# Sparse attention of a two-layer trunk: float32 matmuls replaced by three float16 passes over high and low parts, two heads per pass on the two halves of the rows

## Chip, cores, metric

One core of one Trainium2 chip runs the whole program. The metric is device time in microseconds of one execution, lower is better. Engines are named as in the profile: PE (TensorE matmul), PEld (its weight loads), DVE (VectorE), ACT (ScalarE), POOL (GpSimd), SP (SyncE, which here issues most DMAs).

## The reference, cut to what matters

A trunk of two layers over 512 rows of width 1024, in float32. Each layer has a mixing part with two branches (an RWKV-7 recurrence and a sparse attention), a cross-attention into 256 memory rows, and a feed-forward part (dense in layer 0, 8 experts in layer 1). The change touches the sparse attention alone:

```python
# q: 512 rows x 8 heads x 64, k and v: one head of 64; q_idx: 8 indexer heads x 64, k_idx: 64, w_idx: 8
def query_block(i):                      # 128 queries at a time
    limit = ((start + arange(128)) // 64 + 1) * 64       # keys before limit may be seen
    logits = einsum('bqhd,bsd->bqhs', q_idx, k_idx) * 64 ** -0.5
    score = einsum('bqhs,bqh->bqs', relu(logits), w_idx) * 8 ** -0.5
    score = where(key_pos < limit, score, -1e30)
    sel = top_k(score, 128)              # top_k = min(256, 512 // 4)
    s = einsum('bqhd,bqkd->bqhk', q, k[sel]) * 64 ** -0.5
    p = softmax(where(sel < limit, s, -1e30))
    return einsum('bqhk,bqkd->bqhd', p, v[sel])
```

In the mixing part the recurrence's output and the attention's output are each projected (`w_branch_a`, `w_branch_b`), gated, added and projected again (`w_out`).

## The kernel before

The 512 rows are four tiles of 128 partitions. Weights come in tiles of 512 KB (`raw`), are split into two float16 parts (`whi` by ACT, `wlo` by DVE, line 268, or by POOL, line 266) and multiplied in three float16 passes (high by high, low by high, high by low; `proj_feat`, line 285, tile `pf`, moving 128x512; `proj_tok2`, line 345, tile `ptok`). The recurrence and the sparse attention compute in float32.

**The mixing part** is written as Python generators that `layer` steps through in an order given by a string (`ORDER`): `r` the recurrence, `d` keys and queries, `s` the selection, `a` the attention, `g` gates (16 pf projections), `b` branch projections. A scheduler with a model of the engines then puts the instructions of each engine into their final, static order, so work of all generators is mixed. Every engine runs its own list in that order; an instruction that waits holds up those behind it on the same engine.

**The recurrence** (`rwkv`) handles heads in two groups of four. For each group: `rwkv_mats` (pA, line 793, on PE; AM, line 797, on DVE), `rwkv_inverse` (the block to DRAM and back, `scrA<-AM`, `Bt<-scrA`; a row-by-row inverse on DVE, pr and tt, lines 971 and 972; products pr and z, x, lines 988 and 990; then pY, line 1013, Ys, line 1016, and pX, line 1022), and `rwkv_chain` (pH, pG, pMQ, and then eight steps in which PE computes pSy, line 889, and DVE scales the new state TT, line 897, twice a step; the next step needs TT). `rwkv_out` ends a group (pyT, line 927; pg, line 940; r, line 941). In the trace the second group's inverse follows the first group's chain.

**The sparse attention** (`dsa`). `keys_queries` projects, normalises and rotates, transposes on PE and copies the results out of PSUM into kT, ikT (keys, indexer keys) and qT, iqT (queries). All have 64 numbers per head on the partitions, and two copies or two heads in the two halves of the 128 rows. For each block b of 128 queries, with n = 128 (b+1) keys:
- `select` (b = 1 to 3): per indexer head one matmul pl (line 503, contracting 64 rows, moving n columns), ACT's relu (line 505), DVE's weighted sum into iacc (lines 507, 509); then 16 rounds of top-8 on DVE (MAX8, line 513, and MATCH_REPLACE8, line 514), and the mask (line 515).
- `attend`, called for the two halves jp of the heads and for the parity e of the head: two matmuls psc (line 529), DVE's masked row maximum (line 530), nb (531), ACT's exponential with row sum (534), DVE's rv (536), ACT's scaling (538); after a yield the probabilities are transposed on PE (pp, line 546), copied out (pT, line 547, by ACT or DVE), and multiplied with v (po, line 553). With e = 1 the result is split into ybh, ybl (lines 200, 201) and stored to DRAM (`ybd`). Once all are stored, `branches` loads `yb<-ybd` and runs the pf of `w_branch_b`.

PSUM banks: two are shared by pl, psc, pp and pk (tag `att`), one holds po, two serve pf and ptok.

Of the kernel before, what the change touches and what calls it, by code (L numbers as in the profile page):

```python
# [54 lines left out]
class Kern:  # L55
# [315 lines left out]
    def dsa(self, l, hh, hl, ybd, cx):  # L371
# [68 lines left out]
        def attends():  # L440
            todo = []
            for b in range(NT):
                if b == 0:
                    c2 = ExitStack()
                    dw = pool("dsav", 1, c2)
                if b == 2:
                    next(todo.pop(0), None)
                    c2.close()
                    c1.close()
                    dw = pool("dsaw", 2, cx)  # L450
                for jp in range(2):
                    for e in range(2):
                        todo.append(self.attend(dw, b, jp, e, masks[b], qT, kT, vt, qs, ybd))
                        next(todo[-1])
                        if len(todo) > 1:
                            next(todo.pop(0), None)
# [4 lines left out]

    def queries(self, pp, hh, hl, c, c0, dst, tabs, qs):
# [3 lines left out]
        for cc in range(2):  # L466
            ps = self.proj_tok2([c(c0 + 256 * cc, c0 + 256 * cc + 256)], hh, hl)
            for i in range(2):
# [18 lines left out]
                nc.scalar.copy(dst[:, 2 * cc:2 * cc + 2, 2 * i * P:(2 * i + 2) * P].rearrange("p j (t c) -> p t j c", t=2),  # L487
                               pt.rearrange("p (t j c) -> p t j c", t=2, j=2))

    def select(self, dw, b, m, iqT, ikT, iw):  # L490
# [9 lines left out]
        for h in range(8):  # L500
            hs = slice((h % 2) * 64, (h % 2) * 64 + 64)
            pl = self.bank("att", "pl")
            nc.tensor.matmul(pl[:, :n], lhsT=iqT[hs, h // 2, bs], rhs=ikT[hs, :n], start=True, stop=True)  # L503
# [13 lines left out]
    def attend(self, dw, b, jp, e, mask, qT, kT, vt, qs, ybd):  # L517

        nc = self.nc
        n = (b + 1) * P  # L520
# [4 lines left out]
        mx, nb, sm, rv = (dw.tile([P, 2], F32, name=x, bufs=2) for x in ("mx", "nb", "sme", "rv"))
        q2 = qs[:, b, 4 * jp + e:4 * jp + e + 3:2]
        for i in range(2):
            pl = self.bank("att", "psc")
            nc.tensor.matmul(pl[:, :n], lhsT=qT[es, 2 * jp + i, bs], rhs=kT[es, :n], start=True, stop=True)  # L529
            nc.vector.tensor_tensor_reduce(s2[:, i, :n], pl[:, :n], mask, 1.0, -3.0e38, OP.add, OP.max, mx[:, i:i + 1])  # L530
        nc.vector.scalar_tensor_tensor(nb, mx, -1.0, q2, OP.mult, OP.mult)
        for i in range(2):
            h = 4 * jp + 2 * i + e
            nc.scalar.activation(s2[:, i, :n], s2[:, i, :n], AF.Exp, bias=nb[:, i:i + 1], scale=qs[:, b, h:h + 1],
                                 accum_out=sm[:, i:i + 1])
        nc.vector.reciprocal(rv, sm)
# [3 lines left out]
        pT = dw.tile([P, nm // P, 2 * P], F32, name="pT", bufs=1)  # L540
        for k2 in range(0, b + 1, 2):
            m = min(2, b + 1 - k2)
            pp = self.bank("att", "pp")
            for x in range(2 * m):
                kt = k2 + x // 2
                nc.tensor.transpose(pp[:, x * P:(x + 1) * P], s2[:, x % 2, kt * P:(kt + 1) * P], self.ident)
            (nc.scalar.copy if k2 == 0 else nc.vector.tensor_copy)(
                pT[:, k2:k2 + m, :], pp[:, 0:2 * m * P].rearrange("p (k c) -> p k c", k=m))
        if e == 0:
            self.po = self.bank("po", "po")  # L550
        po = self.po
        for kt in range(b + 1):
            nc.tensor.matmul(po[es, 0:2 * P], lhsT=vt[:, kt, :], rhs=pT[:, kt, :], start=kt == 0, stop=kt == b)  # L553
        if e == 1:
            yh = dw.tile([P, 2, P], F16, name="ybh")
            yl = dw.tile([P, 2, P], F16, name="ybl")
            self.split_ps(yh, yl, po[:, 0:2 * P].rearrange("p (j t) -> p j t", j=2))
            for d, y in zip(ybd, (yh, yl)):
                nc.sync.dma_start(d[2 * jp:2 * jp + 2, :, bs].rearrange("j p t -> p j t"), y)
# [1184 lines left out]
```

## Time and profile before

| what | value |
|---|---|
| median of 3 runs | 2145.76 us (2144.34 to 2150.21) |
| the profiled execution, its own time | 2149.16 us |
| its span in the trace | 2147.3 us |
| mean granted PE clock | 0.96 |
| busy PE, DVE, ACT, POOL | 2006.6, 1379.4, 1011.8, 334.8 us |
| psc (529) on PE, busy | 48.9 us, 128 records of 64 matmuls |
| pl (503) on PE, busy | 50.7 us, 96 records of 48 matmuls |
| po (553) on PE, busy | 44.4 us, 160 records of 80 matmuls |
| pp (546) on PE, busy | 27.7 us, 160 records |

A float32 matmul leaves two records on PE. Busy times of PE overlap, since matmuls are pipelined and their ends are modelled: the distance from one start to the next says what a matmul costs the queue. "Released by" names the work that an engine waited for. The profile's own time exceeds its span by 1.9 us, work outside the trace's first and last instruction.

### The profile page before, as it was taken

Reading aid. Unit: us, or ns where it says so; the run is one execution under the profiler, and the core shown is the slowest. Engines: PE = TensorE matmul, PEld = TensorE weight load, DVE = VectorE, ACT = ScalarE, POOL = GpSimd, SP = SyncE. Lnnn points to the kernel's source line nnn. Section 1 sums busy time; section 2 is a strip of 40 time slices with the busy share of each in tenths; the row PEclk is TensorE's granted clock in tenths of the full one; section 3 lists DMA queues with packets and bytes.
Section 4 is the critical chain, followed back from the end, with each engine's and each line's share of the span. In section 5 each row is a group of like instructions: output and inputs, shape, how many; then the busy total and the mean of one; then the engine's idle time right before and its main releaser. Section 6 shows DMA issues by size and latency. Waiting matters only on the chain.

```text
span 2147.3 us, 40225 instructions
## 1 busy us (share of the span) xinstructions
PE 2006.6 (93%) x16520; PEld 1310.3 (61%) x16520; DVE 1379.4 (64%) x2322; ACT 1011.8 (47%) x1617; POOL 334.8 (16%) x354
## 2 busy tenths in 40 slices
PE   7998999988998999999999988999798799999997
PEld 4664455555464544444583555546455699999996
DVE  6767984555665433322567787464655698888886
ACT  5533344542453333322443344543233488888883
POOL 2261601003010000000252260101100220000002
PEclk9998989999999999999999889999999799999998
DMA  7333323352542333333333231435330899999993
GB/s 226 102 90 83 105 75 90 71 162 88 197 157 63 98 103 104 99 106 100 115 89 84 82 108 48 116 81 178 116 122 27 287 386 374 356 352 344 345 346 120
DMA packets 346706, 332.47 MB, mean 155 GB/s; under 512 B 101889, under 2 KB 263809, under 8 KB 346514
## 3 DMA queue, kind: packets, MB, share of 16 engines
q1 hardware_dynamic: 335408, 306.03, 45.3%
q10 hardware_dynamic: 8482, 15.39, 2.1%
q0 software_dynamic: 2624, 8.40, 1.1%
q8 instruction: 131, 2.15, 0.4%
q14 instruction: 61, 0.50, 0.1%
HBM read 297.05 MB, written 32.72 MB: 154 GB/s over the span
## 4 chain that ended last, share of the span: by engine, by line
PE 70%; DVE 15%; DMA 5%; issue 3%; ACT 2%; SPq 2%; POOL 1%; another core or an unknown queue 0%; ACTq 0%; DVEq 0%; POOLq 0%
PE pf L285 20%; PE pe L1513 12%; PE ptok L327 10%; PE py L1558 6%; PE ptok L345 3%; PE pf L297 3%; PE pSy L889 3%; DVE iacc L514 2%; DVE m L513 2%; DVE wlo L268 2%; PE po L553 1%; PE psc L529 1%; PE pl L503 1%; DVE pr L988 1%; PE pA L793 1%
## 5 line engine op out<-in xcount | busy, mean ns | idle before, releaser
L263 ACT ACTIVATE whi<-raw 128x1024 f16<-128x1024 f32 (+3 forms) x242 | 227.0, 940 | 438.7 <-PE pf L285 195.2
L268 DVE SCALAR_TENSOR_TENSOR wlo<-raw,whi 128x1024 f16<-128x1024 f32 (+3 forms) x208 | 233.7, 1125 | 215.3 <-ACT whi L263 202.4
L1499 DVE SCALAR_TENSOR_TENSOR ewlo<-eraw,ewhi 128x1024 f16<-128x1024 f32 x265 | 321.4, 1222 | 59.4 <-ACT ewhi L1498 58.2
L285 PEld LDWEIGHTS <-whi 128*128 128x128 f16 x1888 | 181.8, 98 | 242.3 <-issue 43.5
L1498 ACT ACTIVATE ewhi<-eraw 128x1024 f16<-128x1024 f32 x265 | 277.2, 1053 | 81.3 <-PE py L1558 34.5
L1513 PE MATMUL pe<-XT,ewhi 128*128 128x144 f16 x2816 | 207.3, 227 | 2.5 <-ACT XT L200 2.3
L1513 PEld LDWEIGHTS <-ewhi 128*128 128x128 f16 x2816 | 184.2, 98 | 3.1 <-issue 2.5
L285 PE MATMUL pf<-hh,whi 128*128 128x512 f16 x448 | 170.8, 381 | 5.6 <-ACT qe L481 2.0
L285 PE MATMUL pf<-hl,whi 128*128 128x512 f16 x448 | 170.9, 382 | 0.0
L285 PEld LDWEIGHTS <-wlo 128*128 128x128 f16 x944 | 92.9, 100 | 113.0 <-issue 12.4
L285 PE MATMUL pf<-fh,whi 128*128 128x512 f16 x336 | 127.3, 379 | 0.0
L285 PE MATMUL pf<-fl,whi 128*128 128x512 f16 x336 | 127.3, 379 | 0.0
L1513 PE MATMUL pe<-XT,ewlo 128*128 128x144 f16 x1408 | 117.7, 227 | 0.2 <-issue 0.2
L285 PE MATMUL pf<-hh,wlo 128*128 128x512 f16 x448 | 116.2, 392 | 0.0
L1558 PE MATMUL py<-HT,ewhi 128*128 128x144 f16 x1408 | 104.0, 227 | 0.0
L164 POOL TENSOR_TENSOR rs<-rs,nrm_e 128x1 f32<-128x1 f32 x28 | 17.5, 625 | 520.4 <-DVE rs L163 520.4
L266 POOL TENSOR_TENSOR wlo<-raw,whi 128x1024 f16<-128x1024 f32 (+3 forms) x34 | 59.2, 1741 | 241.2 <-ACT raw L265 205.2
L1513 PEld LDWEIGHTS <-ewlo 128*128 128x128 f16 x1408 | 95.0, 98 | 0.6 <-issue 0.6
L1558 PEld LDWEIGHTS <-ewhi 128*128 128x128 f16 x1408 | 92.5, 98 | 0.3 <-issue 0.2
L285 PE MATMUL pf<-fh,wlo 128*128 128x512 f16 x336 | 79.4, 379 | 0.0
L345 PE MATMUL ptok<-whi,hh 128*128 128x256 f16 (+1 forms) x320 | 78.8, 285 | 0.0
L345 PE MATMUL ptok<-whi,hl 128*128 128x256 f16 (+1 forms) x320 | 78.5, 284 | 0.0
(435 smaller groups left out, 3863.3 us busy)
## 6 DMA issues: line engine op xcount, KB each, us to landing
raw<-in_w_in_dram SPq DMA_DIRECT2D x76, 512.0 KB
eraw<-in_moe_wg_dram SPq DMA_DIRECT2D x16, 2048.0 KB
eraw<-in_moe_wu_dram SPq DMA_DIRECT2D x16, 2048.0 KB
eraw<-in_moe_wd_dram SPq DMA_DIRECT2D x16, 2048.0 KB
eraw<-in_moe_wg_dram SPq DMA_DIRECT2D x8, 1536.0 KB
eraw<-in_moe_wu_dram SPq DMA_DIRECT2D x8, 1536.0 KB
eraw<-in_moe_wd_dram SPq DMA_DIRECT2D x8, 1536.0 KB
raw<-in_ffn_wg_dram SPq DMA_DIRECT2D x22, 512.0 KB
```

What stands on the lines that cost most here:

```text
L263: nc.scalar.activation(hi, raw, AF.Copy, scale=SW)
L266: nc.gpsimd.tensor_tensor(lo, raw, hi, OP.subtract)
L268: nc.vector.scalar_tensor_tensor(lo, raw, SW, hi, OP.mult, OP.subtract)
L285: self.nc.tensor.matmul(p, lhsT=w[:, k, :], rhs=x[k], start=first, stop=last)
L297: m = self.nc.tensor.matmul(ps[i][:, cs], lhsT=w[:, k, :], rhs=x[k][:, cs], start=hf == 0 and start, stop=stop, skip_group_check=True)
L327: mm(ps[t][:, :N], lhsT=x[:, k0 + k, ts], rhs=w[:, k, :], start=k0 == 0 and first, stop=k0 + kg == kt and last)
L345: mm(p, lhsT=x[:, k0 + k, ts], rhs=w[:, k, :], start=k0 == 0 and t % 2 == 0 and first, stop=k0 + kg == kt and last, skip_group_check=True)
L889: m = mm(p[e][:, cc % 4, jj, :], lhsT=l, rhs=r, start=first[e] is None, stop=x == (1 if cc else 0), skip_group_check=True)
L1498: nc.scalar.activation(r[0], w, AF.Copy, scale=SW)
L1499: nc.vector.scalar_tensor_tensor(r[1], w, SW, r[0], OP.mult, OP.subtract)
L1513: mm(p[:, i * n:(i + 1) * n], lhsT=w[:, k, :], rhs=XT[:, k, h, :], start=z == 0, stop=z == len(ms) - 1)
L1558: mm(ps[d], lhsT=w[:, i, d * P:(d + 1) * P], rhs=HT[:, k, h, :], start=k == 0 and w is wh and h == 0 and d % per == 0, stop=k == FT - 1 an ...
```

## The change

Every operand of the attention's matmuls is kept as two float16 tiles, high and low (`kT[0]`, `kT[1]` and so on), the same bytes as before. `split_ps` writes them: ACT casts the high part out of PSUM, DVE subtracts it and writes the low part. Scores come from a new function `scores` for two heads at once: three passes (high by high, low query by high key, high query by low key), and in each pass one matmul for each parity e, whose 64 rows are the upper or the lower half of the array, into two PSUM banks. `select` uses it for pairs of indexer heads. `attend` handles four heads in one call (both parities); its probabilities are scaled by 64 (`SP`), v by 64 (`SW`), and po is accumulated in three passes with the two parities in turn, each into its half of the output partitions. The tile s2 becomes s4 (four heads, two buffers), pT becomes four float16 tiles.

```diff
-        kT = dp.tile([P, SEQ], F32, name="kT")
-        vt = dp.tile([P, NT, 64], F32, name="vt")
+        two = lambda p, n, *s: [p.tile([P, *s], F16, name=n + x) for x in "hl"]
+        kT = two(dp, "kT", SEQ)
+        vt = two(dp, "vt", NT, 64)
...
-                    nc.scalar.copy(kT[:, cs]..., pv[:, :, 0, :])
-                    nc.vector.tensor_copy(ikT[:, cs]..., pv[:, :, 1, :])
+                    for g, dst in enumerate((kT, ikT)):
+                        self.split_ps(*[d[:, cs]... for d in dst], pv[:, :, g, :])
...
-                nc.scalar.copy(dst[:, 2 * cc:2 * cc + 2, ...], pt...)          # queries: iqT and qT
+                self.split_ps(*[d[:, 2 * cc:2 * cc + 2, ...] for d in dst], pt...)
...
         for h in range(8):                                                     # select
-            pl = self.bank("att", "pl")
-            nc.tensor.matmul(pl[:, :n], lhsT=iqT[hs, h // 2, bs], rhs=ikT[hs, :n], start=True, stop=True)
+            if h % 2 == 0:
+                pls = self.scores(iqT, h // 2, bs, ikT, n)
+            pl = pls[h % 2]
...
+    def scores(self, qT, j, bs, kT, n):
+        pls = [self.bank("att", "psc") for _ in range(2)]
+        for i, (x, y) in enumerate(((0, 0), (1, 0), (0, 1))):
+            for e in range(2):
+                es = slice(e * 64, e * 64 + 64)
+                self.nc.tensor.matmul(pls[e][:, :n], lhsT=qT[x][es, j, bs], rhs=kT[y][es, :n], start=i == 0, stop=i == 2)
+        return pls
...
-            (nc.scalar.copy if k2 == 0 else nc.vector.tensor_copy)(pT[:, k2:k2 + m, :], pp...)
+                self.split_ps(*[t[:, k2:k2 + m, :] for t in pT[e]], pp..., self.SP)
...
-            nc.tensor.matmul(po[es, 0:2 * P], lhsT=vt[:, kt, :], rhs=pT[:, kt, :], start=kt == 0, stop=kt == b)
+            for i, (x, y) in enumerate(((0, 0), (1, 0), (0, 1))):
+                for e in range(2):
+                    nc.tensor.matmul(po[e * 64:e * 64 + 64, 0:2 * P], lhsT=vt[x][:, kt, :], rhs=pT[e][y][:, kt, :],
+                                     start=kt == 0 and i == 0, stop=kt == b and i == 2)
```

The static order changes with it, at three places above all.

DVE, layer 0, where the first recurrence chain begins. Before (line 873, art, ends the chain's preparation; 513 and 514 on 128x512 are the top-8 rounds of block b = 3):

```order
L873 TENSOR_TENSOR art<-pMQ,art 128x512
L530 ISA s_3320,mx<-psc,mask_526 128x128
L530 ISA mx 128x1
L530 ISA s_3320,mx<-psc,mask_526 128x128
L530 ISA mx 128x1
L513 MAX m_2428<-iacc 128x8
L531 SCALAR_TENSOR_TENSOR nb<-mx,qs 128x2
L897 TENSOR_TENSOR TT<-pSy,WC 64x2x64
L514 MATCH_REPLACE iacc<-m_2428,iacc 128x512
L513 MAX m_2431<-iacc 128x8
```

The same place now (TT has line 908, art line 884; the first row is block b = 2's last round):

```order
L514 MATCH_REPLACE iacc<-m_2408,iacc 128x384
L515 TENSOR_SCALAR mask_531<-iacc 128x384
L507 TENSOR_SCALAR iacc<-relu,iw 128x512
L884 TENSOR_TENSOR art<-pMQ,art 128x512
L509 SCALAR_TENSOR_TENSOR iacc<-relu,iw,iacc 128x512
L884 TENSOR_TENSOR art<-pMQ,art 128x512
L509 SCALAR_TENSOR_TENSOR iacc<-relu,iw,iacc 128x512
L908 TENSOR_TENSOR TT<-pSy,WC 64x2x64
L509 SCALAR_TENSOR_TENSOR iacc<-relu,iw,iacc 128x512
```

Seven of block 3's sixteen rounds and all eight of its sums stood ahead of the first TT; now no round and three sums do, and the rest lies between the TTs. In layer 1 the count ahead of the first TT is 10 rounds before and 11 now.

PE, layer 0, second inverse (pY), block b = 3. Before:

```order
L1013 MATMUL pY_3923<-TN_2787,AM_2784 32x32 x15
L546 MATMUL pp_3781<-ct_63,s2_3722 128x128 x4
L553 MATMUL po_3752<-pT_3774,vt_523 64x256 x2
L529 MATMUL psc_3802<-kT_522,qT_525 128x512
L1013 MATMUL pY_3923<-TN_2787,AM_2784 32x32 x17
```

Now (the number behind psc is the bank's tile, so one number is one head):

```order
L523 MATMUL psc_3886<-kTh_522,qTh_527 128x512
L523 LDWEIGHTS qTl_528
L523 MATMUL psc_3886<-kTh_522,qTl_528 128x512
L523 LDWEIGHTS qTh_527
L523 MATMUL psc_3886<-kTl_523,qTh_527 128x512
L560 LDWEIGHTS vth_524
L560 MATMUL po_3856<-pT1l_3831,vth_524 64x256
L523 LDWEIGHTS qTh_527
L523 MATMUL psc_3887<-kTh_522,qTh_527 128x512
L523 LDWEIGHTS qTl_528
L523 MATMUL psc_3887<-kTh_522,qTl_528 128x512
```

The written order alternates the two heads of a pair; in the final order the three passes of one head stand together here, and the partner's follow. Elsewhere (128 and 256 columns above all) the heads do alternate, and the parities of po alternate throughout.

PE, layer 0, where the second recurrence chain meets the branch projection. Before:

```order
L870 MATMUL pMQ<-AM 64x128 x32
L889 MATMUL pSy<-UV,AM 128x64 x2
L285 LDWEIGHTS whi
L285 MATMUL pf<-yb,whi 128x512
L285 LDWEIGHTS whi
L285 MATMUL pf<-yb,whi 128x512
L889 MATMUL pSy<-UV,AM 128x64 x2
```

Now (pSy has line 900):

```order
L560 MATMUL po<-pT1l,vth 64x256
L900 MATMUL pSy<-UV,AM 128x64 x2
L900 MATMUL pSy<-TT,art 128x64 x2
L900 MATMUL pSy<-UV,AM 128x64 x2
L900 MATMUL pSy<-TT,art 128x64 x2
L900 MATMUL pSy<-UV,AM 128x64 x2
L900 MATMUL pSy<-TT,art 128x64 x4
L900 MATMUL pSy<-UV,AM 128x64 x2
L285 LDWEIGHTS whi
L285 MATMUL pf<-yb,whi 128x512
```

The last attention matmuls moved into the second chain, and most of the chain's steps now stand ahead of the first matmul that needs `yb`.

More of the change, by code (lines that the diff above doesn't have):

```diff
@@ L451, in attends @@
                 for jp in range(2):
[L452 to L456, printed above, removed]
+                    todo.append(self.attend(dw, b, jp, masks[b], qT, kT, vt, qs, ybd))
+                    next(todo[-1])
+                    if len(todo) > 1:
+                        next(todo.pop(0), None)
                 yield
@@ L521, in attend @@
         bs = slice(b * P, (b + 1) * P)
-        es = slice(e * 64, e * 64 + 64)
         nm = 2 * P if b < 2 else SEQ
-        s2 = dw.tile([P, 2, nm], F32, name="s2", bufs=2)
-        mx, nb, sm, rv = (dw.tile([P, 2], F32, name=x, bufs=2) for x in ("mx", "nb", "sme", "rv"))
-        q2 = qs[:, b, 4 * jp + e:4 * jp + e + 3:2]
+        s4 = dw.tile([P, 4, nm], F32, name="s4", bufs=2)
+        mx, nb, sm, rv = (dw.tile([P, 4], F32, name=x, bufs=2) for x in ("mx", "nb", "sme", "rv"))
         for i in range(2):
-            pl = self.bank("att", "psc")
-            nc.tensor.matmul(pl[:, :n], lhsT=qT[es, 2 * jp + i, bs], rhs=kT[es, :n], start=True, stop=True)
-            nc.vector.tensor_tensor_reduce(s2[:, i, :n], pl[:, :n], mask, 1.0, -3.0e38, OP.add, OP.max, mx[:, i:i + 1])
@@ L531, in attend @@
[L531 to L535, printed above, removed]
+            for e, pl in enumerate(self.scores(qT, 2 * jp + i, bs, kT, n)):
+                h = 2 * i + e
+                nc.vector.tensor_tensor_reduce(s4[:, h, :n], pl[:, :n], mask, 1.0, -3.0e38, OP.add, OP.max, mx[:, h:h + 1])
@@ L539, in attend @@
         yield
[L540 to L548, printed above, removed]
@@ L549, in attend @@
-        if e == 0:
-            self.po = self.bank("po", "po")
-        po = self.po
-        for kt in range(b + 1):
[L553 to L559, printed above, removed]
+        pT = [[dw.tile([P, nm // P, 2 * P], F16, name=f"pT{e}{x}", bufs=1) for x in "hl"] for e in range(2)]
@@ new lines, in attend @@
+        for e in range(2):
+            for k2 in range(0, b + 1, 2):
+                m = min(2, b + 1 - k2)
+                pp = self.bank("att", "pp")
+                for x in range(2 * m):
+                    kt = k2 + x // 2
+                    nc.tensor.transpose(pp[:, x * P:(x + 1) * P], s4[:, 2 * (x % 2) + e, kt * P:(kt + 1) * P], self.ident)
+                self.split_ps(*[t[:, k2:k2 + m, :] for t in pT[e]], pp[:, 0:2 * m * P].rearrange("p (k c) -> p k c", k=m), self.SP)
+        po = self.bank("po", "po")
@@ L562, in rwkv @@
+        self.split_ps(yh, yl, po[:, 0:2 * P].rearrange("p (j t) -> p j t", j=2), 1 / (SW * self.SP))
+        for d, y in zip(ybd, (yh, yl)):
+            nc.sync.dma_start(d[2 * jp:2 * jp + 2, :, bs].rearrange("j p t -> p j t"), y)
+    SP = 64.0
     def rwkv(self, l, cx, sx, hh, hl, ya):
```

31 lines of the change are left out of this document (19 added, 12 removed).

## Prediction

> **What bounds the kernel now.** I read the page first, then the chain of waits inside the mixing parts of both layers, then busy times by stage, then the distance between matmuls in the timeline.
>
> ```profile
> span 2147.3 us, 40225 instructions
> PE 2006.6 (93%) x16520; PEld 1310.3 (61%) x16520; DVE 1379.4 (64%) x2322; ACT 1011.8 (47%) x1617; POOL 334.8 (16%) x354
> ...
> PE   7998999988998999999999988999798799999997
> ```
>
> PE is the busy engine in nearly every fortieth of the span, which says little about which one holds a given stage. So I cut the mixing parts into stages, by the first and last starts of the recurrence's lines: from the first inverse's end to the first chain (stage 1), first chain (2), second group's matrices and inverse (3), from there to the second chain (4), second chain and tail (5); layer 0, then layer 1.
>
> ```profile
> core 0: us, PE busy (x) PEld busy (x) DVE busy (x) ACT busy (x) POOL busy (x), PEclk, DMA share, GB/s
> 191.00:303.00 112.00, 100.53 (x758) 60.34 (x752) 97.79 (x214) 40.16 (x70) 39.62 (x38) 0.86 0.26 75
> 303.00:361.00 58.00, 58.00 (x341) 34.80 (x342) 32.21 (x94) 30.26 (x75) 7.55 (x4) 0.97 0.31 91
> 361.00:452.00 91.00, 87.11 (x551) 43.74 (x549) 54.86 (x125) 45.16 (x94) 6.07 (x9) 1.00 0.37 89
> 452.00:476.00 24.00, 24.00 (x379) 17.01 (x378) 14.30 (x27) 12.58 (x27) 0.67 (x1) 1.00 0.46 124
> 476.00:541.00 65.00, 53.58 (x336) 31.32 (x333) 35.92 (x69) 17.26 (x41) 18.91 (x14) 0.92 0.39 124
> 1210.00:1310.00 100.00, 89.67 (x661) 53.25 (x662) 82.64 (x174) 38.92 (x71) 40.55 (x38) 0.83 0.28 77
> 1310.00:1367.00 57.00, 55.25 (x350) 32.61 (x351) 31.90 (x92) 28.97 (x73) 5.42 (x3) 0.97 0.34 95
> 1367.00:1458.00 91.00, 90.08 (x558) 45.56 (x558) 54.46 (x126) 45.66 (x95) 6.88 (x10) 1.00 0.38 91
> 1458.00:1481.00 23.00, 21.11 (x387) 15.86 (x381) 12.49 (x22) 10.59 (x21) 1.15 (x1) 1.00 0.57 176
> ```
>
> Stage 1 is DVE's (97.8 of 112 us, 82.6 of 100). Stages 2 to 4 are PE's: 169 of 173 us in layer 0, DVE about 60%. So PE time taken out of stages 2 to 4 can shorten them, and DVE time put into stage 1 lengthens it.
>
> ```profile
> 273.63 1.87 PE pl L503 x2
> ...
> 370.26 0.84 PE psc L529 x2
> ...
> 393.21 2.56 DMA scrA<-AM
> ...
> 447.14 0.62 PE pY L1013 x30
> ...
> 449.35 1.05 PE psc L529 x2
> ...
> 451.09 1.01 PE po L553 x4
> ...
> 462.24 1.02 PE pp L546 x8
> ...
> 468.30 1.87 PE po L553 x8
> ...
> 473.90 6.60 DMA yb<-ybd
> ```
>
> These pieces of the chain (start, length) give prices: one head's psc costs 1.05 us at 512 columns and 0.84 at 384, one key tile of po for both parities 1.01 us, a transposition pp (two records) 0.25. They also show two floors. From 393.21 (the block goes to DRAM) to 447.14 (pY) the second inverse runs through DMA and DVE for 54 us, whatever PE does. And after the last po, pf waits 6.6 us for `yb`.
>
> **The change part by part.** Prices of passes, by starts in the timeline:
>
> ```profile
> 178.13 0.70 PE L503 MATMUL pl<-ikT,iqT 64*128 64x256 f32 x4
> ...
> 302.91 0.48 PE L529 MATMUL psc<-kT,qT 64*128 64x128 f32 x2
> 303.33 1.25 PE L285 MATMUL pf<-hh,wlo 128*128 128x512 f16 x5
> ...
> 325.71 1.13 PE L529 MATMUL psc<-kT,qT 64*128 64x256 f32 x4
> 326.77 1.04 PE L285 MATMUL pf<-hh,wlo 128*128 128x512 f16 x4
> ...
> 445.69 0.38 PE L285 MATMUL pf<-yah,whi 128*128 128x512 f16 x1
> 445.90 0.38 PE L285 MATMUL pf<-yal,whi 128*128 128x512 f16 x1
> ```
>
> A float16 matmul of 512 columns takes 0.21 us of the queue (445.69 to 445.90), so 0.11 at 256. Two float32 heads of 256 columns on the same half of the rows spread over 1.13 us (1.06 from start to the next matmul's, 325.71 to 326.77), two on opposite halves over 0.70: halves do overlap. A float32 record of 512 columns on half the rows takes 0.525 us (1.05/2), where po's records of 256 take 0.234 (1.87/8, so 0.47 at 512): about 0.06 to 0.1 us a record stays uncovered on half rows, which I put down to the weight load. The Trainium skill (TensorE: Matmul & The Clock Gate, Part 3: Packing small matmuls) says that a weight load runs beside a matmul in flight only where the row group differs. By that rule the pf above would show a load between any two; it shows none (0.21 us for 512 columns, each with weights of its own), while psc shows the gap. For passes alone on one half the sum would be 0.3 a pass by the rule and 0.21 by the pf; I take 0.30, since psc is the nearest row.
>
> *Scores (psc).* Before, 16 heads of each width: 16 x (1.05 + 0.84 + 0.53 + 0.42) = 45.4 us. A pass now costs 0.30, 0.25, 0.20 or 0.15 us, for two heads where they alternate in the final order, for one where they don't. By the order about 1, 4, 6 and 5 of the 8 pairs of each width alternate, which makes 44, 36, 29 and 32 passes: 13 + 9 + 6 + 5 = 33 us. Saved 13; ends 2 (no overlap at all) and 24 (all overlap).
>
> *po.* 40 tiles of 1.01 us; now three passes for two parities, between 3 x 0.11 (full overlap) and 6 x 0.11 us. I take 0.5, since no row shows halves of the columns with all rows. Saved 20; ends 14 and 27.
>
> *pl.* Its PE time falls alike, but lies in stage 1, where DVE is the limit. Nothing; its cover is DVE's sums and rounds, and if they were gone the 1.87 us a head at 273.63 would count.
>
> *Splits.* New prices:
>
> ```profile
> L201 DVE TENSOR_TENSOR ql<-pT,qh 128x512 f16<-128x512 f32 x16 | 10.4, 685 | 3.1 <-ACT qh L200 2.9
> ...
> L513 DVE MAX8 m<-iacc 128x8 f32<-128x512 f32 x32 | 22.1, 690 | 0.6
> L514 DVE MATCH_REPLACE8 iacc<-m,iacc 128x512 f32<-128x512 f32 x32 | 21.6, 675 | 0.0
> ...
> L514 DVE MATCH_VALUE_LOAD iacc<-m,iacc 128x8 f32 x96 | 8.3, 86 | 1.6
> ...
> L509 DVE SCALAR_TENSOR_TENSOR iacc<-relu,iw,iacc 128x512 f32<-128x512 f32 x14 | 11.3, 807 | 10.5 <-ACT relu L505 9.7 <-DVE iacc L509 0.5
> ...
> L530 DVE CUSTOM_DVE_ANT_0 s<-psc,mask 128x128 f32<-128x128 f32 x16 | 4.2, 279 | 0.1
> ...
> L536 DVE RECIPROCAL rv<-sme x32: 141/162/167, 297.0 to 1459.1; 128x2 f32<-128x2 f32 x32
> ...
> L547 DVE COPY pT<-pp x16: 415/553/694, 387.6 to 1467.9; 128x256 f32<-128x256 f32 x8, 128x512 f32<-128x512 f32 x8
> ```
>
> Per layer DVE gets 8 splits of queries (0.685 us, 5.5), about 1 of keys and v, and 16 + 8 splits of pT (0.69 and 0.42, 14.4) for 8 copies (4.4); of nb and rv 16 fall away (0.16, -2.5). That is +14 us a layer; ACT gets 8 copies, and has half its time free. A head now also needs its bank until both parts are read (ACT, then DVE).
>
> By stage, with counts from the order:
> - Stage 1, layer 0: seven rounds (0.69 + 0.675 + 0.09 = 1.45), five sums (0.81) and four maxima (0.36) leave DVE's list ahead of the first TT, four query splits come: -10.2 - 4.0 - 1.4 + 2.7 = **-13 us**. Layer 1: one round more, two maxima fewer, four splits: **+3**.
> - Stage 2, layer 0: PE gets 38 pf more (+8.2), block 3's pl (8 heads x 0.9, +7.2), 2.6 us of new psc for 5.4 of old, 2.5 less po, 2 less pp: **+8**; DVE rises by 7 rounds, 5 sums and some splits from 32 to about 50 of 67 and stays under it. Layer 1: 8 pf more (+1.7), psc and po from about 10 to 5, 4 pp fewer: **-5**.
> - Stage 3: up to the second pA about 12 pf fewer and cheaper po: **-5** each. After it the inverse's 54 us cover PE's savings; 12 splits more (8 us of DVE) sit among its DVE steps, whose pauses for DMA hide most: **+3** each.
> - Stage 4: 24 and 20 pf fewer (-5.2, -4.3), po -2.6 and -2, more pp and psc (+2.8, +1.3): **-5** each.
> - Stage 5: the wait for `yb` now follows most of the chain's steps rather than preceding them (6.6 us in layer 0, less in layer 1), against po and pp moved in (+3.5) and 12 pf of `w_branch_b` that now end after pg: **-2** each.
>
> Layer 0: -13 + 8 - 5 + 3 - 5 - 2 = -14. Layer 1: 3 - 5 - 5 + 3 - 5 - 2 = -11. The sum is -25 us: 2149.2 for the profiled execution becomes 2124, and since the median of the runs stands 3.4 us under it, 2121.
>
> **Rivals.**
> - *Hidden anyway.* Stages 3 and 4 are held by the second inverse, and stage 2 by the chain's PE-DVE-PE steps; the PE time saved becomes idle time ahead of pY. For it: the 54 us floor, and attention work that moved into stage 5. Against it: 24.0 of 24 us busy in stage 4. Of the terms stage 1 (-10), block 3's move (+8), the splits (+6) and `yb` (-4) stay: 0, 2146. That the heads of a pair often don't alternate, against what the change says, works the same way.
> - *DVE takes over (slower).* The top-8 rounds now stand between TTs, each 1.45 us, and the pT splits between the inverse's pr and tt. It decides if more than about 24 of the 28 us that DVE gains in both layers are exposed while half of PE's gain is hidden: 28 - 12 = +16, 2160. For it: stage 1's 97.8 of 112. Against: DVE has 36 us free in stage 3.
> - *The clock.* Granted 0.83 and 0.86 in stage 1, where PE waits, and 1.00 in stages 3 and 4, where it is full. With fewer pf as filling, stages 4 and 5 fall to 0.85: about 24 us of matmuls in stage 4 and as many in stage 5 take 15 to 20% more, +5 to +6 a layer, 2132. The Trainium skill (same page, Part 1: The HAM clock gate) has PE drop to half clock after an idle window of about 3.4 us; rows of this case show the lower clock where PE idles, not the window.
> - *More overlap.* Halves overlap and loads are hidden even for passes of one head (0.21), po at its low end: 141 passes by 0.09 and 40 tiles by 0.17 are another -20 in PE time, two thirds of it visible in stages 2 to 4: 2108.
>
> **How the numbers follow.** About 0.3% (6.4 us) is what a measurement of this kernel can tell from no change. Chances: the forecast's own case 0.53 (2110 to 2136), clock 0.10, more overlap 0.08, hidden 0.16, DVE 0.13. An eighth of the hidden case falls beyond 0.3% on each side, so faster 0.73, same 0.12, slower 0.15. The range runs from 2100 (more overlap with all of it visible) to 2152, up to which the hidden case lies; about 0.13 is left above, little below.
>
> **What would show it.** Stage 1 of layer 0 about 13 us shorter, of layer 1 a little longer. psc records of 512 columns 0.3 us apart in threes, alternating pairs at 128 and 256 columns starting together. Six po in 0.4 to 0.6 us. The chain in the second inverse through DMA and DVE, not po and psc. No 6 us piece of `yb` at the head of the second chain. I am wrong if TT waits behind rounds (DVE 95% busy in stage 2), if pY starts no earlier after pA than now, or if PE's clock falls under 0.9 in stages 3 to 5.

## The result, and the profile after

The changed kernel takes 2111.4 us (median of 4 runs, 2107.7 to 2114.5) against 2147.8 before (2144.3 to 2150.2): a ratio of 0.9827, 95% interval 0.9806 to 0.9849, or 36 us. The forecast was 2121, range 2100 to 2152. The two profiled executions stand 41 us apart.

First the page of the changed kernel, then its busy times by the same five stages, layer 0 and layer 1 (columns as in the prediction's table of stages):

```profile
span 2106.0 us, 40672 instructions
PE 1959.0 (93%) x16712; PEld 1294.1 (61%) x16712; DVE 1402.5 (67%) x2346; ACT 1013.8 (48%) x1637; POOL 335.4 (16%) x354
```

```profile
194.60:278.10 83.50, 74.72 (x680) 46.72 (x681) 77.94 (x174) 33.95 (x57) 37.85 (x38) 0.91 0.31 86
278.10:337.30 59.20, 59.20 (x399) 33.91 (x399) 48.64 (x126) 32.08 (x79) 7.49 (x4) 1.00 0.36 107
337.30:429.00 91.70, 80.91 (x587) 41.61 (x587) 61.47 (x137) 47.24 (x105) 6.72 (x10) 0.94 0.44 109
429.00:452.40 23.40, 23.40 (x375) 18.90 (x373) 11.78 (x23) 14.26 (x29) 0.00 (x0) 0.73 0.09 22
452.40:498.00 45.60, 44.69 (x301) 29.48 (x302) 23.77 (x46) 12.02 (x30) 15.57 (x11) 0.89 0.47 148
1184.30:1278.20 93.90, 79.41 (x701) 49.37 (x700) 89.59 (x173) 35.97 (x59) 41.29 (x38) 0.93 0.30 85
1278.20:1331.50 53.30, 51.63 (x362) 32.25 (x362) 32.90 (x94) 31.77 (x85) 5.41 (x3) 0.97 0.39 111
1331.50:1424.60 93.10, 79.07 (x590) 43.19 (x589) 60.98 (x133) 47.89 (x104) 6.72 (x10) 0.91 0.39 100
1424.60:1442.50 17.90, 17.30 (x358) 14.25 (x357) 9.41 (x15) 9.12 (x18) 1.16 (x1) 0.90 0.17 46
1442.50:1488.40 45.90, 45.18 (x295) 29.41 (x296) 23.18 (x48) 11.46 (x30) 14.82 (x14) 0.89 0.45 139
```

Stage 1 of the kernel before, with its edges at the same events (layer 0, then layer 1):

```profile
191.60:302.60 111.00, 99.53 (x734) 59.57 (x734) 97.39 (x212) 39.83 (x69) 39.62 (x38) 0.86 0.26 74
...
1209.90:1310.40 100.50, 90.07 (x665) 53.65 (x665) 83.12 (x175) 38.92 (x71) 40.55 (x38) 0.83 0.27 77
```

PE's busy time fell by 47.6 us and its idle time rose from 140.7 to 147.0; the span lost the difference. But the gain doesn't lie where PE's time was taken out. With the edges set at the same events in both traces (first Ys, first TT, first r), stage 1 of layer 0 went from 111.0 to 83.5 us, and that alone is two thirds of the 41. Stages 3 and 4 of layer 0, where the prediction took 7 us out, went from 115.9 to 115.1, though PE's busy time there fell from 112.0 to 104.3: its saving became idle time and a lower clock.

DVE's busy and idle time in stage 1 say where its 27.5 us went. In layer 0 its busy time fell from 97.4 to 77.9 us and its idle time from 13.6 to 5.6; in layer 1 its busy time rose from 83.1 to 89.6 and its idle time fell from 17.4 to 4.3. So in layer 0 seven tenths of the 27.5 us are work that left DVE's list ahead of the first TT, and the rest, as in layer 1, are waits that went.

What ends the stage is seen in the chain of waits. First before, then the changed kernel's, both from the end of layer 0's stage 1; behind the first a window of the kernel before (columns as above):

```profile
283.05 2.01 PE pl L503 x2
...
285.09 0.61 ACT relu L505
...
285.72 0.76 DVE iacc L509
...
286.69 0.71 DVE m L513
...
298.51 0.61 DVE art L873
...
299.16 0.66 PE pSy L889 x4
```

```profile
274.00:287.00 13.00, 13.00 (x93) 6.70 (x93) 6.12 (x10) 4.46 (x9) 0.00 (x0) 0.50 0.01 3
```

```profile
268.82 1.75 PE pMQ L881 x32
...
273.05 1.89 PE pMQ L881 x32
...
274.94 0.59 PE pSy L900 x4
...
278.12 0.75 PE psc L523 x3
```

Before, all sixteen score records of block 3 stood ahead of pMQ, which the recurrence's chain needs, on PE. The last four heads (pl at 273.63, 276.75, 280.01, 283.05 in the chain) fall into a stretch from 273.9 to 287.5 us in which the granted clock was 0.50. PE is counted busy in all of it; relu and DVE's sums wait for PE, and DVE is busy 6.1 of 13.0 us. In layer 1 it is the same: granted 0.50 from 1277.4 to 1291.0, with block 3's last heads in it. Then, from 286.7 on, the chain is DVE's: block 3's first rounds, with the recurrence's copies and art queued between them, until pSy can start at 299.2. The first pMQ starts at 287.8, the last at 294.5, 103 us into the stage. In the changed kernel 12 of the 24 records are ahead, the clock is at 1.00 from 230.1 us on, the last pMQ starts at 274.7, 80 us into its stage, the first TT 3.4 us later, and the other 12 records run inside the chain. So three things changed together: the records ahead of pMQ on PE, the rounds and sums ahead of TT on DVE, and the clock over block 3's heads.

### The profile page after: what moved, and what is told of

It is laid out like the page before. It is cut to its first block, busy times and chain, and to the rows that moved or that the text cites. A ratio compares the mean times of both kernels' runs of the same rounds, so it can differ in the third digit from the quotient of the medians.

```text
span 2106.0 us, 40672 instructions
## 1 busy us (share of the span) xinstructions
PE 1959.0 (93%) x16712; PEld 1294.1 (61%) x16712; DVE 1402.5 (67%) x2346; ACT 1013.8 (48%) x1637; POOL 335.4 (16%) x354
## 4 chain that ended last, share of the span: by engine, by line
PE 70%; DVE 13%; DMA 6%; ACT 3%; issue 3%; POOL 2%; SPq 2%; ACTq 0%; DVEq 0%; POOLq 0%
PE pf L285 22%; PE pe L1524 12%; PE ptok L327 11%; PE py L1569 6%; PE pSy L900 3%; PE pf L297 3%; PE ptok L345 2%; DVE iacc L514 1%; DVE wlo L268 1%; DVE pr L999 1%; DVE m L513 1%; PE psc L523 1%; PE pmo L1214 1%; DMA eraw<-in_moe_wu_dram 1%; PE pA L804 1%
## 5 line engine op out<-in xcount | busy, mean ns | idle before, releaser
L1510 DVE SCALAR_TENSOR_TENSOR ewlo<-eraw,ewhi 128x1024 f16<-128x1024 f32 x265 | 320.4, 1219 | 58.6 <-ACT ewhi L1509 57.7
L285 PEld LDWEIGHTS <-wlo 128*128 128x128 f16 x944 | 91.4, 99 | 111.9 <-issue 10.0
L266 POOL TENSOR_TENSOR wlo<-raw,whi 128x1024 f16<-128x1024 f32 (+3 forms) x34 | 59.2, 1740 | 283.8 <-ACT raw L265 190.2
L285 PE MATMUL pf<-fh,wlo 128*128 128x512 f16 x336 | 79.4, 380 | 0.0
```

The costliest lines, as they stand in the source:

```text
L266: nc.gpsimd.tensor_tensor(lo, raw, hi, OP.subtract)
L285: self.nc.tensor.matmul(p, lhsT=w[:, k, :], rhs=x[k], start=first, stop=last)
L1510: nc.vector.scalar_tensor_tensor(r[1], w, SW, r[0], OP.mult, OP.subtract)
```

## Experiments

All use the stages above; the table has each run's stages in us, from the same events. "Rounds" counts block 3's top-8 rounds that stand ahead of the first TT in the final order (layer 0/layer 1); "pMQ" is the distance from the start of layer 0's stage 1 to the start of the last pMQ, with the score records of block 3 that start ahead of it. "3+4" is the sum of stages 3 and 4; its last edge lies up to 0.7 us apart between runs, so that differences under 1 us say nothing there. Each ratio is to the kernel before as it was measured beside that run (medians 2147.8 to 2149.9).

| kernel | median | ratio to before (95%) | rounds | pMQ (records ahead) | layer 0: 1, 2, 3+4 | layer 1: 1, 2, 3+4 |
|---|---|---|---|---|---|---|
| before | 2147.8 | | 7/10 | 102.9 (16 of 16) | 111.0, 57.7, 115.9 | 100.5, 56.8, 113.6 |
| changed | 2111.4 | 0.981 to 0.985 | 0/11 | 80.1 (12 of 24) | 83.5, 59.2, 115.1 | 93.9, 53.3, 111.0 |
| e1 before, late | 2122.0 | 0.984 to 0.992 | 0/0 | 92.1 (14 of 16) | 93.0, 61.0, 115.5 | 79.9, 62.1, 113.0 |
| e2 select alone | 2127.5 | 0.987 to 0.994 | 0/8 | 80.7 (15 of 24) | 83.3, 60.6, 123.7 | 88.5, 56.6, 120.7 |
| e3 attend alone | 2126.6 | 0.986 to 0.993 | 3/8 | 90.8 (16 of 16) | 96.9, 54.0, 118.5 | 97.8, 55.3, 107.5 |
| e4 filler | 2100.4 | 0.975 to 0.982 | 0/7 | 80.1 (12 of 24) | 83.5, 59.2, 114.5 | 87.1, 53.2, 107.3 |
| e5 early | 2117.1 | 0.980 to 0.992 | 7/9 | 78.9 (12 of 24) | 107.2, 51.5, 110.3 | 90.5, 53.9, 111.3 |
| e6 changed, late | 2093.5 | 0.970 to 0.981 | 0/0 | 81.3 (12 of 24) | 83.7, 55.2, 113.8 | 79.4, 51.8, 111.9 |
| e7 alternate | 2123.4 | 0.984 to 0.994 | 0/6 | 95.8 (24 of 24) | 97.3, 54.6, 114.9 | 88.5, 54.8, 112.8 |
| e8 attend twice | 2132.0 | 0.991 to 0.997 | 0/10 | 79.9 (12 of 24) | 83.3, 56.0, 115.0 | 95.1, 55.3, 113.5 |
| e9 late, select twice | 2134.7 | 0.989 to 0.996 | 0/0 | 88.3 (22 of 48) | 91.1, 57.9, 123.2 | 82.7, 56.7, 115.5 |
| e10 late, split twice | 2134.1 | 0.991 to 0.996 | 0/0 | 80.2 (12 of 24) | 83.6, 59.0, 125.7 | 77.6, 56.4, 114.0 |
| e11 late, alternate | 2109.3 | 0.979 to 0.984 | 0/0 | 94.9 (18 of 24) | 95.8, 56.2, 114.2 | 80.8, 58.6, 110.1 |
| e12 late, filler | 2118.6 | 0.984 to 0.990 | 0/0 | 78.9 (12 of 24) | 82.3, 54.3, 115.3 | 86.6, 62.5, 113.6 |

**e1: the order alone, in float32.**

```diff
-    ORDER = ("rrrddrrrssrssrrdaagaarra", "rrrddrrsssrrsrrgdaagarraa")
+    ORDER = ("rrrddrrrssrsrsrdaagaarra", "rrrddrrsssrrrsrgdaagarraa")
```

> The kernel before, in float32, with one letter of the written order swapped in each layer: the selection of block 3 is written after the first recurrence chain. In the final order no top-8 round of block 3 and seven of its eight sums stand ahead of the first TT in both layers (before: 7 and 10 rounds, all sums). Theory A (the order made the gain): the changed kernel's stage 1 of layer 0 lost 27.5 us (111.0 to 83.5) because block 3's selection moved behind the first TT; then stage 1 falls here by about 20 us in layer 0 and about 20 in layer 1, part of it comes back in stage 2, and the time is 2110 to 2130 us. Theory B (the price of the float16 selection passes made it): with float32 passes the work is only moved, stage 2 grows by what stage 1 loses, and the time stays within 0.3% of 2147.8.

Measured 2122.0. The first stage fell in both layers, and stage 2 gave back 3.3 and 5.3:

```profile
194.30:287.30 93.00, 84.45 (x691) 52.56 (x692) 84.36 (x176) 36.28 (x60) 39.60 (x38) 0.89 0.28 81
...
1198.70:1278.60 79.90, 72.45 (x627) 44.61 (x627) 66.73 (x129) 33.12 (x55) 38.45 (x38) 0.89 0.31 86
```

Theory A holds: 26 us come from the place of one block's selection, with no float16 in it. Theory B, that work is only moved, fell. By these rows and the ones of the kernel before, 13.0 of the 18.0 us of layer 0's stage 1 and 16.4 of layer 1's 20.6 are DVE's busy time. The rest came with the order too, the clock among it: near block 3's heads the stretch at 0.50 lasts 3.4 us in layer 0, not 13.7.

**e2 and e3: the two halves of the change.** In e2 iqT, ikT and the selection are as in the changed kernel and attend as before; e3 the other way round.

```diff
 # e3, against the changed kernel (e2 is its mirror image against the kernel before)
-            if h % 2 == 0:
-                pls = self.scores(iqT, h // 2, bs, ikT, n)
-            pl = pls[h % 2]
+            hs = slice((h % 2) * 64, (h % 2) * 64 + 64)
+            pl = self.bank("att", "pl")
+            nc.tensor.matmul(pl[:, :n], lhsT=iqT[hs, h // 2, bs], rhs=ikT[hs, :n], start=True, stop=True)
...
```

> The float16 passes in the selection alone; attend, keys and queries of attend as before. In the final order layer 0 has no round of block 3 ahead of the first TT, layer 1 has 8 (before 10). Theory A (order): layer 0's stage 1 about 25 us shorter, layer 1's within 3 us of before; 2120 to 2128 us. Theory B (price of the passes): layer 1's stage 1 also falls by the 6 us that it lost in the changed kernel, and layer 0's by 27; 2112 to 2118 us. Theory C (attend's PE time made the gain): under 8 us in all, above 2140.

> The float16 passes in attend alone; the selection's matmuls in float32 as before. In the final order 3 rounds of block 3 stand ahead of the first TT in layer 0 (before 7), 8 in layer 1 (before 10). Theory A: stage 1 gives 4 x 1.45 = 6 us and 3 us, stages 3 and 4 nothing in layer 0, since the second inverse holds them; 2135 to 2142 us. Theory C (PE time taken out of stages 2 to 4 pays, as the prediction had it, -5 -2 -5 a layer): 2120 to 2130 us.

Measured 2127.5 and 2126.6: 21 and 22 us, together more than the whole change's 36 to 37. Neither fits one theory. In e2 stage 1 fell as in the changed kernel (83.3), but layer 1's fell by 12 with 8 rounds ahead, which A doesn't give, and stages 3 and 4 grew by 7 or 8 in both layers. In e3 the time is the one that theory C gave, but only half its place: layer 1 gained 6 in stages 3 and 4, while layer 0 gained 14 in stage 1 and lost 3 in stages 3 and 4. Stage 1 of layer 0 in e3 is the nearest thing to a test of the clock: all sixteen float32 records stand ahead of pMQ as before, but the granted clock over the last four heads is 1.00 (0.50 only from 268.1 to 271.5), these heads start 1.7 us apart instead of 3.0 to 3.3, and DVE's idle time is 5.6 us, as short as in the changed kernel:

```profile
193.10:290.00 96.90, 87.12 (x704) 52.96 (x705) 91.29 (x196) 37.33 (x62) 40.36 (x38) 0.91 0.29 82
```

That three rounds instead of seven stand ahead of TT changed with it, so this is not a proof. The final order changes everywhere with each edit, so a half's time is not its share.

**e5 and e6: the changed kernel with block 3 early, and late in both layers.** With e1 and the kernel before they make a square: float32 or float16, early or late.

```diff
 # e5, for the first chain of a layer (round7 is the seventh round of the last block selected)
+                    if g == 0 and cc == 0:
+                        self.order(tt.ins, self.round7)
...
 # e6
-    ORDER = ("rrrddrrrssrssrrdaagaarra", "rrrddrrsssrrsrrgdaagarraa")
+    ORDER = ("rrrddrrrssrsrsrdaagaarra", "rrrddrrsssrrrsrgdaagarraa")
```

> The changed kernel with the first two TT of layer 0's first chain tied behind the seventh top-8 round of block 3, as many rounds as stood there before the change. Layer 1's order shifts a little by itself (9 rounds ahead instead of 11). Theory A (order): stage 1 of layer 0 goes from 83.5 back to about 100 us (seven rounds of 1.45, five sums of 0.81, the waits for the heads), stage 2 gives 5 of it back, the time is 2120 to 2126 us. Theory B (the price of the passes alone): stage 1 stays under 88, the time within 4 us of 2111.

> The changed kernel with the written order of the kernel before with the late selection: block 3's selection after the first chain in both layers. Layer 0's order was late already; in layer 1 the rounds ahead of the first TT go from 11 to 0. Theory A: stage 1 of layer 1 falls from 93.9 to about 72 us, stage 2 grows by 5 to 8; 2094 to 2102 us. That is then 20 to 28 us under the float32 kernel in the same order (2122), the part of the gain that belongs to the float16 passes. Rival: float16 gives nothing once the order is the same, 2115 to 2125.

Measured 2117.1 and 2093.5. The first two stages of layer 0 in e5, then stage 1 of layer 1 in e6:

```profile
196.50:303.70 107.20, 98.08 (x803) 56.49 (x801) 96.78 (x218) 46.02 (x81) 40.11 (x39) 0.94 0.33 91
303.70:355.20 51.50, 51.50 (x378) 31.66 (x376) 36.00 (x97) 30.53 (x76) 5.69 (x4) 1.00 0.36 106
```

```profile
1178.40:1257.80 79.40, 68.93 (x670) 43.66 (x672) 72.42 (x141) 34.74 (x58) 40.19 (x38) 1.00 0.38 107
```

In e5 pMQ is as early as in the changed kernel (78.9), but the tied rounds, which need all eight heads' scores first, hold TT, and stage 1 is back at 107.2. So DVE's list alone can end stage 1. But most of the 24 us isn't lost: PE is busy 98.1 of the 107.2 us, and in the last 28 of them the chain of waits runs over PE, two thirds of it pf; stage 2 returns 7.7 us and stages 3 and 4 return 4.8. The time lies between the ranges of the two theories, 6 us above the changed kernel, and the runs of e5 (2109.6 to 2127.1) can't tell that from nothing.

e6 has about the time of theory A, but stage 1 of layer 1 fell to 79.4 and not to 72, and stage 2 didn't grow. By the square, float16 gives 31 us early (2148 to 2117; the interval of e5's ratio has 17 to 44) and 28.5 late (2122 to 2093.5), the late place gives 26 in float32 and 24 in float16. The corners are alike in the written order or in the rounds ahead of TT, not in the whole final order. If the two add, the changed kernel, late in layer 0 and early in layer 1, lies between: 31 by float16 and 6 by the order. e6, 18 us under it, is the best version found.

**e7 and e11: the heads of a pair strictly in turn**, in the changed kernel and in the late one (there with block 3's first round tied behind TT).

```diff
+        last = None
...
+                if last is not None:
+                    self.order(m.ins, last)
+                last = m.ins
```

> The changed kernel with the passes of a pair of heads tied to the alternating order in which they are written (none of the 336 score matmuls follows one of the same head; in the changed kernel 116 do). By the prices in the changed kernel's trace, 0.75 us for the three passes of one head at 512 columns and about 0.004 us from a matmul to its partner on the other half, the eight or so pairs of 384 and 512 columns that don't alternate save 0.6 to 0.75 us each, 12 to 15 us of PE in both layers. If PE's time counts: 2098 to 2105. If stages 3 and 4 are held by the inverse and stage 1 by DVE: 2106 to 2114; order shifts elsewhere (6 rounds ahead in layer 1 instead of 11) can give another 5.

> The late float16 kernel with the passes of a pair tied to the alternating order and block 3's first top-8 round tied behind the first TT, so that 0 rounds stand ahead of it in both layers. In the late kernel 142 of 336 score matmuls follow one of the same head. Theory: the alternation saves about 0.3 us for each such pass of 512 columns and less for shorter ones, 15 us of PE, and the loss of 12 us seen when it was tried in the changed kernel was the order's (all five more sums of block 3 ahead of TT): 2078 to 2088. Rival: both banks are held until the last pass of both heads, DVE and ACT start on a head later, and this eats the gain: 2090 to 2102.

Measured 2123.4 and 2109.3, 12 and 16 us slower than the changed and the late kernel; every expectation missed. (No run has the late kernel with the tied round alone, which e11 and e12 carry too.) Stage 1 of layer 0 is 14 and 12 us longer in both, though no round stands ahead of TT. The chain of waits of e11 shows a part of why:

```profile
281.69 2.50 DVE iacc L509
...
284.21 0.61 ACT relu L505
...
284.86 1.43 PE psc L527 x5
286.29 2.25 PE pf L285 x5
288.54 3.10 PE pMQ L888 x32
```

A tied pair needs both banks free before it can pass, so PE stands idle at psc, for 0.8 and then 2.2 us, until relu has emptied them, and pMQ stands behind it: 18 of 24 records are ahead of the last one (24 in e7), and it starts 95 us into the stage instead of 81. In the loose order, which I had counted as a loss, PE can go on. But 3 us of idle PE are not 12. The larger part is DVE's: its busy time in stage 1 is 86.2 us in e11 against 78.0 in the late kernel (in this order below), and in e7 87.2 against 77.9 in the changed one.

```profile
196.50:292.30 95.80, 84.99 (x721) 51.52 (x721) 86.16 (x179) 38.68 (x63) 42.30 (x39) 0.90 0.32 92
...
198.40:282.10 83.70, 73.84 (x676) 46.57 (x673) 77.99 (x174) 34.02 (x57) 38.05 (x38) 0.91 0.30 86
```

Six (e11) and eight (e7) of block 3's sums stand ahead of TT instead of three, and some take longer, as the 2.50 us above against 0.75 elsewhere; why, the trace doesn't show.

**e4 and e12: idle matmuls in the second inverse**, in the changed kernel and in the late one (with the same tie of block 3's first round).

```diff
+                if fill:                                               # second group; FILL = (1, 1, 2, 4)
+                    for _ in range(self.FILL[2 * (dst is x) + hf]):    # after each half of z and x
+                        nc.tensor.matmul(pY[0:64, :], lhsT=dst[:, hs, :]..., rhs=self.ct[:, 0:512], start=True, stop=True)
...
```

> The changed kernel with idle matmuls added in the second inverse of each layer (their sums are overwritten): float32, 512 columns, 1, 1, 2 and 4 of them after the four halves of z and x, and 2 short ones when the first pieces of the inverse have landed; about 10 to 12 us of PE a layer, where PE has 11 and 14 us idle in stage 3. Theory D (the clock): the granted clock fell to 0.50 for 16 us at the head of stage 4 of layer 0 because PE idled in the inverse before it; with the idle time filled, stage 4 runs at 0.95 or more and takes 16 to 18 us instead of 23.4, layer 1 gains 2 to 4, and the time is 2100 to 2106 us (changed kernel 2111). Rival: the attention's matmuls that the idle ones push back cost as much, 2110 to 2118, whatever the clock.

> The late float16 kernel with the idle matmuls in the second inverse, and block 3's first round tied behind the first TT (0 rounds ahead in both layers). The filled kernel stood 11 us under the changed one, but 7 us of that lay in stage 1 of layer 1, where 7 rounds instead of 11 stood ahead of TT. If idle matmuls by themselves help (clock): 2083 to 2089. If the 11 us were the order's: 2091 to 2099, with the granted clock in stage 4 of layer 0 at 1.00 in both, where the late kernel has 1.00 already.

Measured 2100.4 and 2118.6: 11 us faster than the changed kernel, and 25 slower than the late one. Stages 3 and 4 of layer 0 in e4:

```profile
337.40:424.70 87.30, 82.32 (x581) 40.93 (x580) 57.28 (x128) 44.87 (x100) 6.72 (x10) 0.98 0.43 105
424.70:451.90 27.20, 24.30 (x408) 18.19 (x407) 16.70 (x34) 16.72 (x34) 0.00 (x0) 1.00 0.18 49
```

e4's time is the one that theory D gave, but not by its mechanism. The clock did what the theory said (1.00 instead of 0.73 in stage 4, where the changed kernel has 0.50 for the first 12.7 us), yet stage 4 takes 27.2 us instead of 23.4, not 16 to 18, and the two stages together gave about 1 us. The two profiles stand 8 us apart. Layer 1's stage 1, where 7 rounds instead of 11 are ahead of TT, gave 7 us, its stages 3 and 4 gave 4, with stage 4 at 0.67, and its stage 5 gave 5; but 252 pf come after its r instead of 204, 10 us. e12 lies above both its cases: its stage 4 of layer 0 has 1.00, and layer 1's stages 1 and 2 are 18 us longer than the late kernel's. What the idle matmuls do by themselves is not shown; the order that came with them weighs more.

**e8, e9, e10: one suspected cost doubled.** e8 repeats attend's score passes, e9 the selection's in the late kernel, e10 DVE's writing of the low part of pT in the late kernel.

```diff
 # e8, e9
-        for i, (x, y) in enumerate(((0, 0), (1, 0), (0, 1))):
+        for i, (x, y) in [p for _ in range(reps) for p in enumerate(((0, 0), (1, 0), (0, 1)))]:     # reps = 2
...
 # e10, in attend; the second call leaves out ACT's high part
-                self.split_ps(*[t[:, k2:k2 + m, :] for t in pT[e]], pp..., self.SP)
+                for _ in range(2):
+                    self.split_ps(*[t[:, k2:k2 + m, :] for t in pT[e]], pp..., self.SP, _)
```

> The changed kernel with the three score passes of attend done twice (the second round starts the sums anew), which adds to PE what the scores cost, about 14 us a layer by the trace, and changes nothing else but the order that the scheduler makes of it (layer 0: 0 rounds ahead of TT as before; layer 1: 10). If PE's time in stages 2 to 4 counts in full: +28, 2139. If half of it is hidden by the second inverse: 2120 to 2128. If all of it is: 2108 to 2114, or less, if it holds the clock up.

> The float16 kernel with the late selection (2093.5 us, 0 rounds of block 3 ahead of the first TT in both layers, and 0 here), with the three passes of the selection's scores done twice. In the changed kernel's trace these matmuls take about 31 us of PE's queue in both layers. Theory P (PE's queue is what the whole mixing part is short of, whatever stage its work lies in; the doubled scores of attend cost 21 us for 19 us of queue): 2118 to 2126. Theory S (stage 1 is DVE's, as the prediction had it, and the selection's PE time is free there): 2093 to 2100.

> The same late float16 kernel, with the low part of each transposed probability tile written twice by DVE: 24 more operations a layer of 0.69 and 0.42 us, 14.4 us a layer, 29 us in both; PE's work is unchanged. If DVE's time is on the path (rival 'DVE takes over'): half to all of it, 2108 to 2122. If it stands beside PE's work in stages 3 and 4: 2092 to 2099.

Measured 2132.0 (+21), 2134.7 (+41) and 2134.1 (+41); e9 and e10 lie above all their cases. e8 lies between its cases, and shows where hidden PE time goes: stages 3 and 4 of layer 0 keep their 115.0, but 239 and 262 pf matmuls start after the second group's first r, where the changed kernel has 179 and 204 (those of `w_branch_b` went from 12 to 72 in each layer). Float16 pf at 0.21 us each, 118 more of them, are 25 us. PE time added beside the inverse pushes pf behind it. The change itself didn't pull any forward the other way: in layer 1 192 pf came after that r before, 204 in the changed kernel. In e10 stages 3 and 4 of layer 0 grew by 12 with PE's work unchanged,

```profile
339.50:432.20 92.70, 75.16 (x562) 39.84 (x561) 64.47 (x142) 47.02 (x103) 6.56 (x10) 0.90 0.43 105
432.20:465.20 33.00, 31.63 (x407) 22.42 (x408) 19.07 (x36) 14.60 (x31) 0.00 (x0) 0.72 0.04 9
```

and 288 pf instead of 221 come after the r of layer 1. So splits of pT in the inverse can cost much more than the +3 a layer that the prediction had for them, if the order that came with the edit isn't the cause. How much each doubling costs by itself stays open: both exceed what was added (25 us of PE's queue by the starts in the changed kernel's trace, where the expectation's 31 had counted waits, and 29 of DVE), and e11 and e12 stand 16 and 25 us above the late kernel, one with no more work and one with the idle matmuls and the tie of a round.

## Why the prediction was right, and where it wasn't

The direction was right, and the time, 10 us under the forecast, lay in the range. The steps were near in their prices and often wrong in their places.

**Prices.** The timeline of the changed kernel shows one head's three passes of 512 columns, then six po, then two heads of 256 columns in turn:

```profile
401.49 0.39 PE L523 MATMUL psc<-kTh,qTh 64*128 64x512 f16 x1
401.71 0.38 PE L523 MATMUL psc<-kTh,qTl 64*128 64x512 f16 x1
401.93 0.38 PE L523 MATMUL psc<-kTl,qTh 64*128 64x512 f16 x1
...
338.54 0.30 PE L560 MATMUL po<-pT0h,vth 128*64 128x256 f16 x1
338.55 0.30 PE L560 MATMUL po<-pT1h,vth 128*64 128x256 f16 x1
...
338.79 0.27 PE L560 MATMUL po<-pT1l,vth 128*64 128x256 f16 x1
338.99 0.28 PE L523 MATMUL psc<-kTh,qTh 64*128 64x256 f16 x2
339.11 0.27 PE L523 MATMUL psc<-kTh,qTl 64*128 64x256 f16 x2
```

A pass of one head costs 0.22 us, not 0.30: the pf row was the right neighbour and the float32 psc the wrong one. Pairs in turn do overlap: of the 60 pairs in the trace that start within 0.013 us of each other, 38 are 0.003 or 0.004 us apart. Added up from start to next start, attend's psc went from 44.1 to 29.5 us (predicted 45.4 to 33) and po from 41.2 to 21.5 (predicted 40.4 to 20). By the Trainium skill (TensorE: Matmul & The Clock Gate, Part 3: Packing small matmuls) a weight load runs beside a matmul in flight only where the row group differs, though the same section also lets it run ahead into a background weight buffer. These passes share a row group, each with weights of its own, and at 0.22 us from start to start show no load, so the rule in its short form doesn't hold here. The same section's 4 ns between starts on different row groups agrees with the pairs here.

**"pl: nothing, its cover is DVE's sums and rounds"** is the step that failed. The prediction read stage 1 from DVE's busy share (97.8 of 112, 82.6 of 100) and costed DVE's list alone, -13 and +3; DVE's waits in the stage, 13.6 and 17.4 us, it put at nothing. Measured were -27.5 and -6.6. DVE's busy time went by -19.5 and +6.5, the right way and half as much again or more as the terms have it, and its idle time by -8.0 and -13.1, for which there was no term. 10 of these 21 us are the sums' waits for relu, so for the heads (4.5 to 1.6 us in layer 0, 8.8 to 1.7 in layer 1). The pl row of the chain that the prediction quoted itself (273.63, 1.87 us for one head) was the hint: it ran at a granted clock of 0.50. How much of the waits belongs to the clock, to cheaper passes and to the records' place ahead of pMQ stays open: e3 has the old place at a granted 1.00 and short waits, e7 and e11 have more records ahead and longer waits (10.1 and 9.6 us).

**Stage 2** of layer 0, +8, measured +1.5. pf grew as foreseen (37 more against 38), and DVE's 48.6 us of work stayed under the stage. But of block 3's eight heads at 0.9 us (+7.2) only half run inside the chain, 12 records at 0.22 us, 2.6 us. Stage 2 of layer 1, -5: -3.5.

**Stages 3 and 4**, -7 a layer, measured -0.8 and -2.6. Divided at the second group's last pA and at the first pY, the terms did better than their sum. Up to the last pA they got 7.9 and 5.0 us shorter (forecast 5); from there to pY, in the inverse, 4.2 and 3.3 longer (forecast 3, for the splits); stage 4 got 0.4 and 4.5 shorter (forecast 5). A piece with no term, from pY to Ys, got 3.3 and 3.7 longer; there the granted clock was 0.55 and 0.52, 1.00 before. So the rival "hidden anyway" was right about the inverse: pY starts no earlier after the last pA than before, one of the signs named for being wrong. PE's savings ahead of the inverse did show.

**Stage 5**, -2 each: -2.1 and -0.4; the wait for `yb` moved into the chain, and shrank from 6.6 us:

```profile
462.38 3.92 DMA yb<-ybd
```

Not foreseen at all: 3 us more up to the first Ys, in a part that the prediction left out.

**The clock** was 0.73 in stage 4 of layer 0 and 0.89 in stage 5 of both layers, below the 0.9 named as a sign for being wrong, and yet the time wasn't longer. The late kernel's stage 4 has 1.00 and takes 24.4 us, e4's has 1.00 and takes 27.2, the changed kernel's has 0.73 and takes 23.4; from pY to the first TT the late kernel takes 31.1 us and the changed one 32.6. The mechanism of that rival was there; a cost of more than 2 us isn't shown. What the rival didn't look at is stage 1 of the kernel before, where a low clock that the change took away may be a part of the gain.

So the profiled -41 against the forecast's -25 is two errors of opposite sign: stages 1 and 2 of both layers gave 29 us more than their terms (-36 instead of -7), stages 3 and 4 gave 11 less (-3 instead of -14). That the sum came as near as it did is in part luck.

## What to carry to other kernels

An engine that is 87% busy in a stage still waits for 13% of it: price its list and its waits apart, and for each wait look for what the other engine is doing then and at which granted clock. A change that a static scheduler rearranges is two changes, a price and an order; try the order alone first, here one swap of letters in each layer, 26 us. Six float16 kernels of nearly the same work (the changed one, e5, e6, e7, e11, and e4 with its idle matmuls) lie between 2093 and 2123, so one pair of kernels cannot tell a price of 10 us.

## What the runs showed of the hardware

Here the granted clock fell after 4 us in which PE was nearly idle, and came back 20 us later. Windows of 2 us of the changed kernel, before pY and at the end of the stretch (columns as above):

```profile
416.00:418.00 2.00, 0.37 (x4) 0.20 (x2) 1.62 (x3) 2.00 (x7) 0.00 (x0) 1.00 0.55 91
418.00:420.00 2.00, 0.22 (x2) 0.00 (x0) 0.77 (x2) 2.00 (x6) 0.00 (x0) 1.00 0.55 140
420.00:422.00 2.00, 0.85 (x16) 0.54 (x18) 1.02 (x2) 2.00 (x5) 0.00 (x0) 0.80 0.67 145
422.00:424.00 2.00, 2.00 (x41) 1.55 (x36) 0.00 (x0) 0.72 (x2) 0.00 (x0) 0.50 0.58 115
...
440.00:442.00 2.00, 2.00 (x31) 1.60 (x31) 1.38 (x2) 0.73 (x3) 0.00 (x0) 0.58 0.00 0
442.00:444.00 2.00, 2.00 (x48) 1.80 (x45) 0.23 (x1) 0.96 (x3) 0.00 (x0) 1.00 0.04 8
```

PE is busy 0.6 of 4 us, then runs at 0.50 for 20.5 us (421.2 to 441.7), in which it is counted as busy throughout. In the 14 traces such stretches last 3.41 us or a whole multiple of it, but for the one that each trace ends in; in the changed kernel's trace 9 of 22 last 3.41 us, and this one, of 6 times that, is the longest. The Trainium skill (TensorE: Matmul & The Clock Gate, Part 1: The HAM clock gate) has half clock after an idle window of about 3.4 us, which agrees, and full clock after one busy window of the same length, which doesn't in this stretch: here it took six times that.
